# Moving 32 of 48 modulation blocks from VectorE and GpSimd into TensorE steps of a later scan

## The chip, the cores and the metric

One core of one Trainium2 chip runs the whole program. The metric is device microseconds of one execution; lower is better.

## The reference, cut to what matters

The program is two blocks of a network over 1024 tokens of width 1024. The first block has two layers (dilated attention beside a gated scan, then an HGRN scan). The second block is modulated by a condition vector, mixes a pooled branch, an SSD scan and a delta-rule scan (GDN), and ends in 16 experts. The modulation rows are what the change is about:

```python
sc = jax.nn.silu(c)              # c: 1 x 1024
scc = jax.nn.silu(c_ctx)[None]
m_lat = jnp.split(sc @ ada_w[l] + ada_b[l], 6, axis=-1)    # ada_w: 1024 x 6144
m_ctx = jnp.split(scc @ ada_w[l] + ada_b[l], 6, axis=-1)
h_lat = modulate(rms_norm(x, norm1_g[l]), m_lat[0], m_lat[1])
h_ctx = modulate(rms_norm(ctx, norm1_g[l]), m_ctx[0], m_ctx[1])
...
x = x + m_lat[2][:, None] * mix_lat
h_lat = modulate(rms_norm(x, norm2_g[l]), m_lat[3], m_lat[4])
x = x + m_lat[5][:, None] * expert_choice_ffn(h_lat, ...)
```

Columns 0 to 2047 of `ada_w` (shift and scale of the first norm) are needed for both condition vectors and early, by the context; columns 2048 to 6143 are needed for `c` alone and not before the mixers' output projection.

## The kernel before, in words

The kernel is written with a tile framework. The program text gives each instruction a priority by its place (earlier text first; `high_priority` lifts a stretch), and a planner puts the ready instruction of highest priority next on each engine's in-order queue, by its own estimate of durations. So work that stands later in the text runs early where it is ready, as filler. Tiles live in pools on a left and a right stack; a pool opened after another has closed takes its memory. Tiles of one tag share `bufs` buffers. PSUM banks are tags too: in the second block there are three banks `mm`, one `a`, two `o` and two `tr`.

The order of the text: the four heads of layer 0 (`Layer0.heads`, with `Gated` units on all engines and dense products of three passes, `mm3`, L135 to L141); after head 3, two `inputs` pieces and `modulation()`, which runs `ada`; then attention, the output projection, the context, HGRN with the context's work aside, the second projection; then `latent_mixers`: projections, `ssd`, three `gdn_scan` pairs hp = 0, 1, 2; then `MixersOut` in four groups, the router and the experts.

`ada` (L939) makes the 6144 columns in 48 blocks of 128. A block has two loads `aw` of 256 KB (L955, two buffers, 512-byte pieces). Where `j % 3 != 2` (two blocks of three), GpSimd scales the four k-slices by `c` (L966) and adds them up (L967, L969, L972); else VectorE does it in four accumulating instructions (L961, L963). The first 16 blocks do this for `c_ctx` too, always on VectorE. One TensorE product with a column of ones sums over the partitions (L978, PSUM tag `f` while `aside` is set), VectorE adds the bias (L979), and a store writes 128 columns to `mods` in DRAM (L980).

`gdn_scan` prepares both directions and returns `carry`, which walks 15 steps: eight small products into the one bank `a` (L1702) and one VectorE addition (L1704), each step waiting for the last, at high priority. `gdn_finish` (L1727) normalises, transposes, gates and stores. All text of `scan(0)` and of `ssd` stands before the first `carry`. The pools `ls` (SSD's tiles) and `lphs` close after `ssd`; `MixersOut.open` then opens `z2` in their place: `z` (8 x 4 KB per partition), `m2` from `mods`, weights and the inputs `yin`. A group of `MixersOut` is 96 products of 512 columns (8 token blocks x 2 halves x 2 chunks x 3 passes) and 16 additions into `z` (L1911).

## Time and profile before

| what | us |
|---|---|
| runs shown | 3608.28, 3609.12, 6455.0 |
| median of the runs | 3609.12 |
| the profiled execution | 3603.5 |
| its span, first to last instruction | 3601.4 |
| TensorE busy | 3217.0 (89%) |
| VectorE / ScalarE / GpSimd busy | 2527.6 / 1577.9 / 1383.2 |
| modulation, first to last load issue | 10.8 to 566.8 |
| SSD's last store and first load of MixersOut | 3011.9 and 3013.3 |

All stretches are in us from the start of the span. PE is TensorE's products, PEld its weight loads, DVE is VectorE, ACT ScalarE, POOL GpSimd, SP the engine that issues most DMAs. The row PEclk is the clock granted to TensorE as a share of full speed. Busy products overlap in TensorE's pipeline, so start-to-start distances are the better price of one.

### The profile page before, as it was taken

Reading aid. Unit: us, or ns where it says so; the run is one execution under the profiler, and the core shown is the slowest. Engines: PE = TensorE matmul, PEld = TensorE weight load, DVE = VectorE, ACT = ScalarE, POOL = GpSimd, SP = SyncE. Lnnn points to the kernel's source line nnn. Section 1 sums busy time; section 2 is a strip of 40 time slices with the busy share of each in tenths; the row PEclk is TensorE's granted clock in tenths of the full one; section 3 lists DMA queues with packets and bytes.
Section 4 is the critical chain, followed back from the end, with each engine's and each line's share of the span. In section 5 each row is a group of like instructions: output and inputs, shape, how many; then the busy total and the mean of one; then the engine's idle time right before and its main releaser. Section 6 shows DMA issues by size and latency. Waiting matters only on the chain.

```text
span 3601.4 us, 63422 instructions
## 1 busy us (share of the span) xinstructions
PE 3217.0 (89%) x23688; PEld 2585.4 (72%) x23688; DVE 2527.6 (70%) x5574; ACT 1577.9 (44%) x3344; POOL 1383.2 (38%) x1415
## 2 busy tenths in 40 slices
PE   7998898999979999999999989869897777849997
PEld 6887786766658878788887877656676666637765
DVE  4777664346685686987668677758996665578876
ACT  3444333544424454545546452235342432126765
POOL 4657673000043233433324331443222564335533
PEclk9999999999999999999999999879998888969999
DMA  5233344252343222111112234234345755668994
GB/s 183 77 92 92 95 130 144 80 190 75 100 140 99 64 68 58 55 60 52 41 49 68 66 134 136 82 88 120 103 131 142 168 148 173 230 193 317 378 348 156
DMA packets 374000, 461.27 MB, mean 128 GB/s; under 512 B 150419, under 2 KB 280723, under 8 KB 373692
## 3 DMA queue, kind: packets, MB, share of 16 engines
q1 hardware_dynamic: 359852, 407.93, 36.3%
q0 software_dynamic: 13840, 49.29, 4.4%
q8 instruction: 187, 3.06, 0.4%
q14 instruction: 121, 0.99, 0.1%
HBM read 357.57 MB, written 104.27 MB: 128 GB/s over the span
## 4 chain that ended last, share of the span: by engine, by line
PE 49%; DVE 22%; DMA 9%; issue 8%; POOL 7%; ACT 3%; SPq 2%; DVEq 0%; POOLq 0%; ACTq 0%
PE mm L139 10%; PE mm L140 9%; PE mm L141 9%; POOL aw L966 2%; PE a L249 2%; DVE cacc L1145 2%; PE a L406 1%; PE a L2041 1%; DMA aw<-in_ada_w_dram 1%; DMA srow<-rdsl 1%; PE a L141 1%; PE a L140 1%; PE o L225 1%; PE a L139 1%; POOL wlo L116 1%
## 5 line engine op out<-in xcount | busy, mean ns | idle before, releaser
L116 POOL TENSOR_TENSOR wlo<-wraw,whi 128x1024 fp32r<-128x1024 f32 (+1 forms) x131 | 328.3, 2510 | 525.6 <-ACT whi L115 513.2
L139 PE MATMUL mm<-x1h,whi 128*128 128x512 f32 x576 | 234.9, 408 | 3.3 <-DVE G L921 1.7
L140 PE MATMUL mm<-x1l,whi 128*128 128x512 f32 x576 | 233.4, 405 | 1.7 <-DVE x1l L133 1.7
L141 PE MATMUL mm<-x1h,wlo 128*128 128x512 f32 x576 | 233.5, 405 | 0.0
L139 PE MATMUL mm<-whi,x1h 128*128 128x256 f32 x768 | 221.8, 289 | 0.4 <-DVE G L921 0.4
L141 PE MATMUL mm<-whi,x1l 128*128 128x256 f32 x768 | 219.6, 286 | 0.0
L140 PE MATMUL mm<-wlo,x1h 128*128 128x256 f32 x768 | 219.0, 286 | 0.0
L2029 DVE TENSOR_TENSOR elo<-eraw,ehi 128x1024 fp32r<-128x1024 f32 x136 | 184.8, 1381 | 47.1 <-ACT ehi L2027 46.7
L2027 ACT CAST ehi<-eraw 128x1024 fp32r<-128x1024 f32 x160 | 165.5, 1051 | 99.6 <-PE a L141 35.9
L115 ACT CAST whi<-wraw 128x1024 fp32r<-128x1024 f32 (+1 forms) x131 | 136.1, 1040 | 153.9 <-PE mm L140 76.2
L140 PE MATMUL mm<-wlo,xh 128*128 128x256 f32 x640 | 184.2, 288 | 1.9 <-POOL wlo L116 1.9
L141 PE MATMUL mm<-whi,xl 128*128 128x256 f32 x640 | 184.4, 289 | 0.0
L139 PE MATMUL mm<-whi,xh 128*128 128x256 f32 x640 | 183.6, 288 | 0.9 <-DVE G L623 0.9
L139 PE MATMUL mm<-x2h,whi 128*128 128x512 f32 x400 | 166.9, 417 | 10.2 <-ACT cu L1134 5.6
L139 PE MATMUL mm<-whi,yin 128*128 128x512 f32 x352 | 151.4, 433 | 25.0 <-DVE z L824 14.0
L141 PE MATMUL mm<-x2h,wlo 128*128 128x512 f32 x400 | 164.3, 412 | 0.8 <-POOL wlo L116 0.8
L140 PE MATMUL mm<-x2l,whi 128*128 128x512 f32 x400 | 164.6, 411 | 0.0
L139 PE MATMUL mm<-xh,whi 128*128 128x512 f32 x336 | 138.6, 412 | 20.4 <-ACT whi L115 17.6
L966 POOL TENSOR_SCALAR aw<-aw,ac 128x128 f32<-128x128 f32 x256 | 123.7, 498 | 85.7 <-DMA aw<-in_ada_w_dram 41.6
L139 PEld LDWEIGHTS mm<-whi,x1h 128*128 128x128 f32 x768 | 146.7, 191 | 3.1 <-issue 1.0
L140 PEld LDWEIGHTS mm<-wlo,x1h 128*128 128x128 f32 x768 | 146.7, 191 | 0.6
L141 PEld LDWEIGHTS mm<-whi,x1l 128*128 128x128 f32 x768 | 146.8, 191 | 0.3
(747 smaller groups left out, 10317.0 us busy)
## 6 DMA issues: line engine op xcount, KB each, us to landing
eraw<-in_we_gate_dram SPq DMA_DIRECT2D x64, 512.0 KB
eraw<-in_we_up_dram SPq DMA_DIRECT2D x64, 512.0 KB
eraw<-in_we_down_dram SPq DMA_DIRECT2D x64, 512.0 KB
yin<-yd POOLq DMA_DIRECT2D x29, 1024.0 KB, 9.6
aw<-in_ada_w_dram SPq DMA_DIRECT2D x96, 256.0 KB
yd<-y_hl SPq DMA_DIRECT2D x80, 256.0 KB
wraw<-in_w_dram SPq DMA_DIRECT2D x25, 512.0 KB
wraw<-in_w_out_dram SPq DMA_DIRECT2D x24, 512.0 KB
```

The lines of the kernel that those rows point to most:

```text
L115: nc.scalar.copy(hi[:, :sz], raw[:, :sz])
L116: nc.gpsimd.tensor_tensor(lo[:, :sz], raw[:, :sz], hi[:, :sz].bitcast(F32), op=ALU.subtract)
L139: nc.tensor.matmul(ps, sh, mh, start=first and i == 0, stop=False)
L140: nc.tensor.matmul(ps, sh, ml, start=False, stop=False)
L141: nc.tensor.matmul(ps, sl, mh, start=False, stop=last and i == n - 1)
L225: nc.tensor.matmul(up[:, :Vd], kdT[:, i * P:(i + 1) * P], V[:, gi, :], start=True, stop=True)
L249: nc.tensor.matmul(ap[32 * c:32 * c + 32, o + lo:o + hi], sta[:, o + 32 * c:o + 32 * c + 32], mov[:, o + lo:o + hi], start=True, stop=True)
L406: nc.tensor.matmul(Ss[h][:, i * 256:i * 256 + w], q[hs[h], qc:qc + P], k[hs[h], lo:lo + w], start=True, stop=True)
L966: nc.gpsimd.tensor_scalar(w[:, k], w[:, k], at(k), 0.0, op0=ALU.mult, op1=ALU.add)
L1145: nc.vector.scalar_tensor_tensor(acc, u[:, i:i + n], cw[:, i:i + 1], acc, op0=ALU.mult, op1=ALU.add)
L2027: nc.scalar.copy(hi, raw)
L2029: nc.vector.tensor_sub(lo, raw, hi.bitcast(F32))
```

## The change

`ada` keeps the 16 blocks that both vectors need. The other 4096 columns move to a new generator `ada_rest`: 8 blocks of 512 columns, 8 k-steps each. A step loads 128 x 512 of `ada_w` (256 KB, 2 KB pieces, eight buffers) and issues four products, one per 32-column tile of the array: the stationary side is `c`'s slice in column 0 of a zeroed 128 x 32 tile, the moving side 128 columns of the weights, and tile q writes PSUM partitions 32q to 32q + 31. After eight steps one VectorE addition over 128 x 128 adds the bias, and one store writes 512 columns from partitions 0, 32, 64 and 96. `silu_c` (a load, three ScalarE and two VectorE instructions on 128 x 16) is now run in both places.

The generator is advanced one or two steps ahead of each step of `carry`, 22 times per scan, 66 in all for its 64 steps. Its pool `adb` is opened after `ls` and `lphs` have closed and is closed before `MixersOut` opens `z2`; the bank of its sums is `mm`.

```diff
+def ada_rest(g, pool, out):
+    nc, I = g.nc, g.I
+    c = silu_c(g, pool)
+    cz = pool.tile([P, 8, 32], F32, name="acz")
+    nc.vector.memset(cz, 0.0)
+    nc.vector.tensor_copy(cz[:, :, 0], c[:, 0])
+    b = pool.tile([P, P], F32, name="ab")
+    nc.vector.memset(b, 0.0)
+    for j in range(4, 12):
+        ps = g.psum("mm")[:, :P]
+        nc.sync.dma_start(b[0::32], dap(I["ada_b"], [[P, 4], [1, P]], j * 512))
+        for k in range(8):
+            w = pool.tile([P, 512], F32, name="aw", tag="aw", bufs=8)
+            nc.sync.dma_start(w, I["ada_w"][:, k, j * 512:(j + 1) * 512])
+            for q in range(4):
+                nc.tensor.matmul(ps[32 * q:32 * q + 32], cz[:, k], w[:, q * P:(q + 1) * P], start=k == 0, stop=k == 7)
+            if k < 7:
+                yield
+        r = pool.tile([P, P], F32, name="ar", tag="ar", bufs=2)
+        nc.vector.tensor_add(r, ps, b)
+        nc.sync.dma_start(dap(out, [[P, 4], [1, P]], j * 512), r[0::32])
+        yield
...
-    for j in range(6144 // n):
-        both = j < 2048 // n
+    for j in range(2048 // n):
...
-    def carry():
+    def carry(side=()):
+        side = iter(side)
...
         for i in range(m if fin is not None else m - 1):
+            for _ in range(1 + i % 2):
+                next(side, None)
             ps = g.psum("a")
...
-        for hp in range(3):
-            then = scan(hp + 1) if hp < 2 else None
-            gdn_finish(g, hp_, carry(), hp, fm_out["g", hp], Y)
-            carry = then
+        with g.pool("adb") as ap:
+            side = ada_rest(g, ap, z.mods)
+            for hp in range(3):
+                then = scan(hp + 1) if hp < 2 else None
+                gdn_finish(g, hp_, carry(side), hp, fm_out["g", hp], Y)
+                carry = then
+            for _ in side:
+                pass
         z.open()
```

## Rows read from the trace of the kernel before

**Rows 1.** Busy time of each engine by stage; columns as its first line says.
```profile
core 0: us, PE busy (x) PEld busy (x) DVE busy (x) ACT busy (x) POOL busy (x), PEclk, DMA share, GB/s
100.00:250.00 150.00, 149.59 (x1199) 128.47 (x1197) 120.03 (x333) 66.24 (x149) 84.31 (x114) 1.00 0.29 87
250.00:575.00 325.00, 294.65 (x2305) 247.45 (x2305) 220.09 (x574) 127.71 (x301) 232.23 (x363) 0.96 0.34 104
575.00:615.00 40.00, 29.25 (x149) 22.07 (x148) 15.83 (x37) 11.12 (x31) 12.87 (x12) 0.84 0.39 118
2770.00:3013.00 243.00, 175.78 (x2101) 155.83 (x2102) 156.57 (x268) 90.44 (x187) 145.65 (x122) 0.81 0.66 153
3013.00:3026.00 13.00, 9.22 (x169) 8.18 (x168) 7.64 (x16) 4.57 (x10) 9.56 (x8) 0.87 1.00 325
3026.00:3040.00 14.00, 8.35 (x85) 6.32 (x85) 4.73 (x12) 1.14 (x2) 0.00 (x0) 0.74 1.07 406
3013.00:3119.00 106.00, 82.18 (x665) 65.02 (x664) 58.27 (x100) 16.22 (x29) 33.38 (x28) 0.87 0.69 224
3119.00:3180.00 61.00, 60.45 (x346) 47.17 (x346) 34.53 (x75) 19.52 (x44) 21.64 (x22) 1.00 0.54 212
```

**Rows 2.** The chain that ended last in 250 to 575, shares by line.
```profile
by line: POOL aw L966 18.5%; DMA aw<-in_ada_w_dram 13.8%; issue 10.1%; DVE aacc L963 5.1%; PE mm L139 5.0%; PE mm L140 4.5%; PE mm L141 4.4%; POOL aw L967 4.4%; POOL wlo L116 3.0%; POOL aacc L972 2.7%; POOL aacc L969 2.3%; POOL u_qh L239 2.
```

**Rows 3.** Busy time in 250 to 575: tile `aw`'s instructions, then line L978's alone.
```profile
250.00:575.00 325.00, 40.83 (x96) 155.61 (x286) 0.96 0.34 104
...
250.00:575.00 325.00, 13.11 (x68) 3.04 (x68) 0.96 0.34 104
```

**Rows 4.** What TensorE waited for in 250 to 575: total us, times, longest.
```profile
PE a L214 <- DVE u_kd L210: 7.1, 5, 2.9
PE f L978 <- POOL aacc L972: 4.6, 5, 1.4
PE a L249 <- POOL u_qh L239: 4.5, 5, 2.6
...
PE f L978 <- POOL qdb L241: 0.8, 1, 0.8
PE f L978 <- DVE aacc L963: 0.5, 1, 0.5
```

**Rows 5.** Tile `aw` over the whole span: ns min/median/max, first and last start.
```profile
L966 POOL TENSOR_SCALAR aw<-aw,ac x256: 363/374/2561, 21.1 to 562.9; 128x128 f32<-128x128 f32 x128
```

**Rows 6.** SP's issues in order of time, 3010 to 3022.
```profile
3011.88 1.39 SPq L1355 DMA_DIRECT2D yd<-shl  x3
3013.31 0.50 SPq L1881 DMA_DIRECT2D m<-mods  x1
3015.50 6.07 SPq L1904 DMA_DIRECT2D z<-x2d  x8
```

**Rows 7.** The chain that ended last, 240 to 620: start, us, what.
```profile
376.05 1.94 DMA mods<-ar
378.34 2.80 DMA aw<-in_ada_w_dram
```

**Rows 8.** TensorE in order of time, 549.1 to 550.1: column tiles, then full-array products.
```profile
549.44 0.36 PE L249 MATMUL a<-u_qh,u_kh 128*32 128x64 f32 x6
549.73 0.50 PE L141 MATMUL mm<-xh,wlo 128*128 128x512 f32 x1
550.07 0.40 PE L139 MATMUL mm<-xh,whi 128*128 128x512 f32 x1
```

**Rows 9.** The chain that ended last, 2760 to 3110: eight fp32 products of 128x128 by 128 columns.
```profile
2870.53 2.00 PE tr L1649 x8
```

**Rows 10.** TensorE in 3013 to 3119 by line: busy, mean ns, idle before.
```profile
L139 PE MATMUL mm<-mhi,yin 128*128 128x512 f32 x76 | 32.3, 430 | 12.8 <-DMA yin<-yd 12.0 <-ACT mhi L1897 0.6 <-DVE z L1911 0.2
```

**Rows 11.** TensorE in order of time: products of MixersOut, then steps of scan 2.
```profile
3028.67 0.39 PE L140 MATMUL mm<-mlo,yin 128*128 128x512 f32 x1
3028.90 0.40 PE L141 MATMUL mm<-mhi,yin 128*128 128x512 f32 x1
3033.99 0.70 PE L1702 MATMUL a<-hB,hA 64*64 64x64 f32 x8 [0.40 <-DVE hB L1704]
3035.09 0.70 PE L1702 MATMUL a<-hB,hA 64*64 64x64 f32 x8 [0.40 <-DVE hB L1704]
```

**Rows 12.** GpSimd and SP in order of time, around 2755 and 2773.
```profile
2755.92 1.81 POOL L1528 MEMSET hwb<- 128x2048 f32 x1 [0.97 <-DVE gH L1492]
...
2773.15 0.34 SPq L1518 DMA_DIRECT2D gT<-gR  x1
```

More of the change, by code (lines that the diff above doesn't have):

```diff
@@ L936, with silu_c @@
 EPS2 = 1e-6
+def silu_c(g, pool):
+    c = pool.tile([P, 2, 8], F32, name="ac")
+    sg = pool.tile([P, 2, 8], F32, name="acs")
+    g.nc.sync.dma_start(c, g.I["c2"])
+    sigmoid(g, sg, c)
+    g.nc.vector.tensor_mul(c, c, sg)
+    return c
+def ada_rest(g, pool, out):
[20 more added lines that the diff above has]
+        yield
 def ada(g, pool, out):
     nc, I = g.nc, g.I
-    c = pool.tile([P, 2, 8], F32, name="ac")
-    sg = pool.tile([P, 2, 8], F32, name="acs")
-    nc.sync.dma_start(c, I["c2"])
-    sigmoid(g, sg, c)
-    nc.vector.tensor_mul(c, c, sg)
+    c = silu_c(g, pool)
     ones = pool.tile([P, 1], F32, name="aones")
@@ L949, in ada @@
     n = 128
-    for j in range(6144 // n):
-        both = j < 2048 // n
-        acc = [pool.tile([P, n], F32, name=f"aacc{v}", tag=f"aacc{v}", bufs=1) for v in range(1 + both)]
+    for j in range(2048 // n):
+        acc = [pool.tile([P, n], F32, name=f"aacc{v}", tag=f"aacc{v}", bufs=1) for v in range(2)]
         for kh in range(2):
@@ L955, in ada @@
             nc.sync.dma_start(w, I["ada_w"][:, 4 * kh:4 * kh + 4, j * n:(j + 1) * n])
-            for v in ((1, 0) if both else (0,)):
+            for v in (1, 0):
                 at = lambda k: c[:, v, 4 * kh + k:4 * kh + k + 1]
@@ L972, in ada @@
                         nc.gpsimd.tensor_add(acc[v], acc[v], w[:, k])
-        for v in range(1 + both):
+        for v in range(2):
             r = pool.tile([1, n], F32, name="ar", tag="ar", bufs=1)
```

## The prediction, as it was put on record

> **What bounds the kernel now.** TensorE is busy for 3217 of 3601 us, so the first view is the table of stages, read for where TensorE is not busy and who is. Beside the modulation it shows two pictures [rows 1]: full from 100 to 250 (149.6 of 150 us), but 30.4 us idle from 250 to 575, with GpSimd at 71%. In this second part all 32 blocks that the change moves are made. The chain of waits there runs through them: GpSimd's scaling, the loads and the additions of `aw` make some 47% of it [rows 2]. A chain share is no gain, since TensorE is 91% busy beside it, so the third view is what TensorE itself waited for [rows 4]: 5.9 us for the modulation's sums, and 7.1 and 4.5 us for `u_kd` and `u_qh`, which VectorE and GpSimd make between modulation instructions. Where the work goes, TensorE is 72% busy and the DMA engines 66% from 2770 to 3013, while SSD and the scans run; from 3119 to 3180 TensorE is full [rows 1]. What starts the last stretch is the order of loads: SSD's last store, then at once `m2`, the weights and `z` [rows 6].
>
> **Early part, what goes.** In 250 to 575 `aw` costs GpSimd 155.6 us and VectorE 40.8 us, and L978 costs TensorE 13.1 us in 68 instructions [rows 3]. Nearly all is moved work (32 products of two instructions are 64 of the 68). Sure is the product time, 13.1 x 64/68 = 12.3 us, and the 5.9 us of waits on these sums. Of the other 24.5 us of idle I take a quarter, 6 us: the waits for `u_kd` and `u_qh` (11.6 us) have two causes, the queue of their engine and the length of their own chain, and I give the queue half. Sum 24 us. Ends: 8 us, if the gated units' chain sets the end, as from 575 to 615, where TensorE idles 10.8 of 40 us with no modulation product left but one [rows 1]; and 12.3 + 30.4 = 43 us if all idle time goes.
>
> The scaling instruction takes 374 ns in the median, but up to 2561 ns, and 155.6 us over 286 instructions of `aw` is far above the median [rows 3, 5]: GpSimd is held up while VectorE works. The Trainium skill (SBUF — State Buffer, section "SBUF: two separate sides") says why: GpSimd and a VectorE instruction with two SBUF inputs use one port pair under an exclusive lock, held for a whole instruction. By that rule VectorE gets back what it waits as well, and the early gain would go towards its upper end, 43 us; no row here separates VectorE's wait for a lock from its work.
>
> Removed at no gain: 64 loads and 64 small transfers from SP's queue, and 16.8 MB from a stage whose DMA share is 0.34 [rows 1]; the first 250 us keep their work.
>
> **Late part, what comes.** 64 loads of 256 KB (16.78 MB), 256 products, which are 512 instructions as fp32 takes two, 8 additions, 8 bias loads, 8 stores. When can they start? Memory is waited for tile by tile: `hwb`, a tile of the scans' pool, was cleared at 2755.9, once the one old tile beneath it had been read, 17 us before the last store from the same old pool [rows 12]. But `adb` lies where SSD's tiles lie, and, by the order of tiles in the text, most of its eight load buffers cover tiles that SSD reads to its last chunks. `z2` lies there too, and all its loads came after SSD's last store, at 3013 [rows 6]. I take 3013 for `adb` as well.
>
> Then the loads set the pace. Two neighbouring stretches with saturated DMA moved 325 and 406 GB/s [rows 1], so 16.78 MB take 52 or 41 us; I take 46. A load's latency (2.8 us), and the last block's addition and store (a `mods` store took 1.9 us), make 5 us [rows 7]. Other loads that run in the same stretch (before, 13 us at 325 and 14 us at 406 make 9.9 MB, less `z`'s 4.2 MB) cost 6 of some 15 us that they would need alone, as most wait for `m2`. `ada_rest` ends at 3013 + 46 + 5 + 6 = 3070.
>
> Its products beside that: six on column tiles took 0.29 us from first start to the next other product [rows 8], 0.05 us each, so 512 take 25 us, under the loads. The upper end is the full-array price, 2.00/8 = 0.25 us [rows 9], 128 us in all. I take the first, since it is the same 128x32 form. The additions (0.3 us), clearing `cz` and `ab`, and the second `silu_c` lie beside the first loads; without that cover they would cost 5 us.
>
> Who waits: on SP an `aw` load waits for the products eight loads before it, and behind it stand the scans' `hS` and gate loads and the stores of `gdn_finish`. On TensorE a product waits for its load, and behind it stand the steps of scan 2, 1.1 us each [rows 11]; 15 steps, some 17 us, fit into the 57 us. On the bank side a sum holds one of three `mm` banks for eight steps. The heavy wait is a new one: `z` lies over `adb`, so it can't be loaded before `ada_rest` is done, and no sum of MixersOut can leave PSUM before.
>
> What the end then is: MixersOut's 384 products start 0.23 us apart [rows 11], 89.5 us. By 3119 the old kernel had done 3 x 76 = 228 of them [rows 10]; the other 156 are 36.4 of the 60.5 us busy in 3119 to 3180 [rows 1], leaving 24.1 us for transposes and router. From 3070: 2.5 us until `z`'s first tile, 89.5 + 24.1 us, less three banks done ahead (18 x 0.23 = 4.2 us), plus 6 us for imperfect packing. That ends at 3188, against 3180. Only 8 us are lost, as the old kernel idles TensorE for 24 of 106 us from 3013 [rows 1]; the scan steps move into the wait. What is late next is the choice of experts and their products, unchanged and shifted.
>
> **Sum.** 3603.5 - 24 + 8 = 3587.5 in the profiled run's terms. The median of the runs shown is 5.6 us above that execution, so the forecast is 3593 us.
>
> **Rivals.** *The loads crawl* (slower). `z` is held by `ada_rest`'s end, so every microsecond of loading beyond 3070 is lost in full. The late part eats the early gain when it ends at 3086, with 62 us for the loads, 16.78 MB at 271 GB/s. For it: the stages around moved 153 and 212 GB/s [rows 1], though not for lack of bandwidth in the second, and the expert weights may be fetched as soon as the scans' memory is free, ahead of `z`. Against it: the two saturated stretches. At 212 GB/s the loads take 79 us: 33 us more, 3626 us. At 153 GB/s, 110 us, it is 3657.
>
> *Blocks hide inside SSD.* One or two buffers cover tiles that SSD frees early, and waits go tile by tile [rows 12]. If most blocks are done by 3013, the late part costs nothing but crowding: 3585 us, and less if TensorE's idle time there shrinks. Against: all of `z2`'s loads waited for SSD's last store [rows 6].
>
> *The early stage doesn't shrink.* The gated units' chain sets its end, gain 8 us: 3609 us. For it: VectorE's chain instructions are no fewer, and 10.8 us idle remain at its tail. Against: the full stage from 100 to 250, with the same chain.
>
> *Four tiles are no four.* The products run one after another at the full-array price: 128 us instead of 46, 82 us more, 3675 us. Against: the column-tile rows [rows 8].
>
> *Changing the shape costs.* After column tiles, the first full-array product of the trace starts its successor 0.34 us later instead of 0.23 [rows 8, 11], 0.11 us; two changes per generator step, 128 in all, make 14 us, 3607 us if none hides under loads. The Trainium skill (TensorEngine Tiling (Array Packing), "Key Properties") says that a change of tiling mode drains TensorE, and here 128x32 tiles would alternate with the scans' 64x64 and MixersOut's full array; by its rule the price stands at every change, by the trace it is 0.11 us.
>
> **How the numbers follow.** Chances: forecast 0.42, loads crawl 0.22, hidden in SSD 0.14, no early gain 0.14, shape 0.05, tiles in a row 0.03. The likeliest one's own range is 3575 to 3611 (41 to 52 us of loads, early gain 14 to 30). The whole range is 3564 to 3642: below, the early gain's upper half with the forecast's late part, or hidden blocks; above, the middle of the crawling loads. A measurement of this kernel tells 2% (72 us) from no change: below 3537 needs the whole 43 us early and as much late (0.02); above 3681 needs the loads at the bottom rate and no early gain (0.04); within it 0.94.
>
> **What would show it.** Right: in the changed profile TensorE idles at most 15 us over what is left of the stage now at 250 to 575, attention starts some 24 us earlier, `aw` loads of 256 KB run back to back for about 50 us right after SSD's last store, and `z`'s first load comes right behind the last `mods` store. Wrong: loads of `aw` well before SSD's end; a stretch in which TensorE waits for `aw` with scan steps queued behind; `z` loaded more than 75 us after SSD's last store; or an attention start that hasn't moved. The forecast fails most easily by the planner: a new order on SP or TensorE in stages that the change doesn't touch.

## The result, and the profile after

| | before | after |
|---|---|---|
| median of the runs, us | 3609.12 | 3629.27 |
| ratio after / before | | 1.0072, 95% interval 1.0058 to 1.0087 |
| the profiled execution, its span | 3603.5, 3601.4 | 3629.27, 3627.5 |
| attention's first instruction (tile `spread` is cleared) | 611.1 | 569.8 |
| SSD's last store | 3012.8 | 2967.1 |
| last modulation store of `ada_rest` | | 3042.8 |
| MixersOut: first and last sum into `z` | 3046.8, 3171.6 | 3065.8, 3195.5 |
| experts: first one-hot tile | 3230.9 | 3255.2 |

The kernel became slower by 0.7%, 26 us by the ratio (20 between the two medians): clear of the spread, though less than 2%. One disturbed run of before (6455) stands outside the ratio. SSD's last store is the last of three; the 3011.9 given ahead of the prediction is the first of them. The table tells where: a lead of 41 us at attention, 46 us at SSD's end, and a lag of 24 us at MixersOut's last sum, which stays to the end. So 70 us are lost between 2967 and 3196, more than the early part wins.

**The early part.** Busy time by stage, in the columns of [rows 1]. The stretch from 250 to 575 now ends at 535:

```profile
core 0: us, PE busy (x) PEld busy (x) DVE busy (x) ACT busy (x) POOL busy (x), PEclk, DMA share, GB/s
250.00:535.00 285.00, 274.39 (x2242) 240.19 (x2241) 157.30 (x451) 127.17 (x298) 99.29 (x90) 0.98 0.18 59
535.00:571.00 36.00, 24.78 (x136) 19.05 (x135) 15.27 (x36) 11.66 (x33) 9.11 (x11) 0.85 0.32 107
```

TensorE's idle time fell from 30.4 to 10.6 us and its busy time by 20.3, together the 40 us. What it still waits for there, the first two of four lines (total us, times, longest), against [rows 4]:

```profile
PE tr L314 <- DVE s_y L291: 7.0, 3, 3.4
PE a L214 <- DVE u_kd L210: 1.7, 3, 1.0
```

The waits for `u_kd` fell from 7.1 to 1.7 us, and that for `u_qh` is gone. More happened than a shorter queue: the same VectorE instructions became shorter. Groups of VectorE by line, before (250 to 575) and after (250 to 535), busy and mean ns:

```profile
L187 DVE TENSOR_TENSOR u_kb<-u_b 128x256 f32<-128x256 f32 x21 | 12.4, 591 | 0.5
L180 DVE TENSOR_TENSOR_SCAN u_b<-reset,gm 128x256 f32<-128x256 f32 x12 | 11.0, 917 | 0.3
```
```profile
L187 DVE TENSOR_TENSOR u_kb<-u_b 128x256 f32<-128x256 f32 x20 | 8.5, 425 | 0.7
L180 DVE TENSOR_TENSOR_SCAN u_b<-reset,gm 128x256 f32<-128x256 f32 x11 | 7.6, 690 | 0.3
```

One form on one tile takes 591 ns in the mean beside a GpSimd that is busy for 71% of the stage, and 425 beside one at 35%. The mean hides how it comes about. The same line before, ns min/median/max:

```profile
L187 DVE TENSOR_TENSOR u_kb<-u_b x21: 404/426/2433, 250.5 to 557.4; 128x256 f32<-128x256 f32 x21
```

The median is the same as after; a few instructions take much longer, one of them 2433 ns (the other 20 have a mean of 499). In the trace, the six of the 21 with no GpSimd instruction beside them took 406 to 425 ns, with as much DMA traffic around them as the others had; all nine above 426 ns had one beside them, and six that had one were not slower. The Trainium skill (SBUF — State Buffer, section "SBUF: two separate sides") states the lock between the two engines that the prediction weighed; these rows agree with it. The gain came near the upper end of 43 us, though not by the sum that gave that end, since 10.6 us of idle time remain.

**The late part.** SP's issues in order of time, against [rows 6]:

```profile
2964.05 3.51 SPq L1386 DMA_DIRECT2D yd<-shl  x6
...
2969.62 0.43 SPq L964 DMA_DIRECT2D aw<-in_ada_w_dram  x1
...
3042.78 0.49 SPq L971 DMA_DIRECT2D mods<-ar  x1
3043.33 0.43 SPq L1919 DMA_DIRECT2D m<-mods  x1
...
3045.44 2.50 SPq L1942 DMA_DIRECT2D z<-x2d  x5
...
3080.86 0.90 SPq L2059 DMA_DIRECT2D eraw<-in_we_gate_dram  x2
...
3097.93 37.33 SPq L1933 DMA_DIRECT2D mraw<-in_w_out_dram  x6
```

The order is the one foretold: late loads right behind SSD's last store, `m2` and `z` right behind the last modulation store. The sizes are not: 73 us from the first late load to the last modulation store, and the last six weight loads of MixersOut stand behind 14 loads of expert weights (3081 to 3097). The tile `aw` over the span (ns min/median/max, first and last start), and who waited for it (us, times):

```profile
L966 PE MATMUL mm<-aw,acz x512: 272/297/423, 2973.8 to 3042.1; 128*32 128x128 f32 x171
...
L964 SPq DMA_DIRECT2D aw<-in_ada_w_dram x64: 327/382/1524, 2969.6 to 3035.9; - x64
...
PE mm L966: 14.7, 23
```

Busy time by stage of the late part, then pieces of it: one amid the late loads, the others through MixersOut:

```profile
2967.10:3042.80 75.70, 58.25 (x1039) 38.54 (x1040) 22.27 (x53) 8.94 (x21) 11.10 (x8) 0.80 0.87 292
3042.80:3195.50 152.70, 121.80 (x580) 93.62 (x577) 77.03 (x124) 25.32 (x47) 43.10 (x38) 0.89 0.56 201
...
2985.00:3005.00 20.00, 13.54 (x228) 8.54 (x228) 4.50 (x9) 2.32 (x4) 1.50 (x3) 0.63 1.04 372
...
3043.00:3060.00 17.00, 7.52 (x67) 4.99 (x62) 7.01 (x7) 2.65 (x4) 6.59 (x4) 0.75 0.91 339
3060.00:3080.00 20.00, 16.29 (x59) 12.34 (x59) 11.10 (x18) 3.25 (x6) 5.83 (x5) 0.78 0.85 258
3080.00:3100.00 20.00, 13.24 (x55) 10.22 (x54) 13.32 (x22) 2.38 (x4) 6.51 (x6) 0.90 0.97 340
3100.00:3120.00 20.00, 12.14 (x39) 9.14 (x39) 5.93 (x9) 1.24 (x2) 2.88 (x2) 0.76 0.62 224
3120.00:3140.00 20.00, 16.91 (x67) 13.38 (x68) 8.73 (x13) 1.14 (x2) 3.96 (x4) 0.92 0.37 132
3140.00:3160.00 20.00, 20.00 (x89) 16.52 (x88) 11.45 (x17) 1.24 (x2) 2.56 (x2) 0.99 0.00 1
```

TensorE stands idle for 31 of the 153 us from the last modulation store to the last sum, all of it ahead of 3140, and its clock is at 0.75 to 0.92 there. What it waited for between 3045 and 3140, and then the chain that ended last, in order of time:

```profile
PE mm L139 <- ACT mhi L1935: 10.2, 2, 5.9
PE mm L139 <- DVE z L1949: 8.6, 6, 2.5
PE mm L139 <- DMA yin<-yd: 8.4, 2, 5.3
```
```profile
3052.16 9.52 DMA mraw<-in_w_out_dram
...
3085.57 12.28 DMA eraw<-in_we_up_dram
3097.93 14.59 DMA mraw<-in_w_out_dram
...
3130.92 5.34 DMA yin<-yd
```

The chain reads as the queue does: a weight load that shares the DMA engines with `z`, then an expert load, then a weight load of 14.59 us behind the expert loads, then inputs. These last inputs were not issued before 3130.92 because their buffer was not free: GpSimd, which issues them, stood 13.9 us for TensorE's products (`PE mm L141`). So part of this chain is MixersOut's own buffers and not the queue.

### The profile page after: what moved, and what is told of

It reads as the page before. It is cut to its first block, busy times and chain, and to the rows that moved or that the text cites. A ratio compares the mean times of both kernels' runs of the same rounds, so it can differ in the third digit from the quotient of the medians.

```text
span 3627.5 us, 63825 instructions
## 1 busy us (share of the span) xinstructions
PE 3229.6 (89%) x24136; PEld 2595.5 (72%) x24136; DVE 2481.9 (68%) x5467; ACT 1579.9 (44%) x3347; POOL 1245.1 (34%) x1142
## 4 chain that ended last, share of the span: by engine, by line
PE 56%; DVE 20%; DMA 9%; issue 7%; POOL 3%; ACT 3%; SPq 2%; DVEq 0%; POOLq 0%; ACTq 0%
PE mm L139 11%; PE mm L140 11%; PE mm L141 11%; PE a L249 2%; DVE cacc L1176 2%; DMA aw<-in_ada_w_dram 1%; PE o L225 1%; PE a L406 1%; PE a L2079 1%; PE a L140 1%; PE a L141 1%; DVE elo L2067 1%; DMA srow<-rdsl 1%; PE a L139 1%; DVE gtmp L1496 1%
## 5 line engine op out<-in xcount | busy, mean ns | idle before, releaser
L141 PE MATMUL mm<-x1h,wlo 128*128 128x512 f32 x576 | 232.4, 404 | 0.0
L141 PE MATMUL mm<-whi,x1l 128*128 128x256 f32 x768 | 219.6, 286 | 0.0
L141 PE MATMUL mm<-whi,xl 128*128 128x256 f32 x640 | 182.8, 286 | 0.0
L239 POOL TENSOR_TENSOR u_qh<-u_qa,facY 128x256 f32<-128x256 f32 x64 | 68.1, 1064 | 293.4 <-DVE u_qa L236 272.0
L141 PE MATMUL mm<-x2h,wlo 128*128 128x512 f32 x400 | 163.0, 408 | 0.8 <-POOL wlo L116 0.8
L239 POOL TENSOR_TENSOR u_qh<-u_qa,facX 128x256 f32<-128x256 f32 x64 | 67.0, 1046 | 245.5 <-DVE u_qa L236 193.7
```

The source lines that it names most:

```text
L141: nc.tensor.matmul(ps, sl, mh, start=False, stop=last and i == n - 1)
L239: nc.gpsimd.tensor_tensor(v3(qh, 32), v3(qa, 32), bcast(fqh, nck, 32), op=ALU.mult)
```

## The experiments

Each stands beside fresh runs of the kernel before. Theory A, as first written: MixersOut's start is held by the late part (its memory lies over `adb`, its loads stand behind the late ones), and TensorE has used up the scan steps that covered that start. Theory B: the bytes moved between SSD's last store and MixersOut's third group set the time. Theory C: the planner loses the early gain on the way. Theory D: the 512 products are the price.

**Early half alone.**

```diff
-        with g.pool("adb") as ap:
-            side = ada_rest(g, ap, z.mods)
...
+    nc.sync.dma_start(dap(out, [[4096, 1], [1, 4096]], 2048), dap(I["ada_b"], [[4096, 1], [1, 4096]], 2048))
```

> The early half alone: the 32 blocks are gone from the early part and nothing takes their place late; the 4096 late columns of the modulation get their bias only, by one transfer, so their products are left out. Theory A (the early gain is whole and the loss is all late): TensorE enters attention 40 us earlier, as in the changed kernel, and keeps it to the end, 3609 - 40 = 3569 us, between 3563 and 3573. The forecast's own term: 24 us, 3585. Theory C (the early gain is lost again on the way, by a new order of the planner): over 3600.

Measured: 3577.69 us beside 3605.59, ratio 0.992 (0.9899 to 0.9942): 29 us. In its trace attention starts 39 us earlier and SSD's last store is 36 us earlier, but MixersOut's last sum only 23:

```profile
L1946 DVE TENSOR_TENSOR z<-z,mm x64: 673/687/690, 3012.2 to 3148.4; 128x512 f32<-128x512 f32 x64
...
L1737 PE MATMUL a<-hB,hA x336: 217/219/367, 2825.7 to 3059.9; 64*64 64x64 f32 x168
...
3104.52 0.61 PE L2225 MATMUL o<-rw,shb 128*128 128x16 f32 x2 [12.21 <-DVE shb L2224]
```

The scans' last step, the second line, in the kernel before and in the changed one:

```profile
L1702 PE MATMUL a<-hB,hA x336: 218/267/367, 2846.3 to 3060.1; 64*64 64x64 f32 x168
```
```profile
L1736 PE MATMUL a<-hB,hA x336: 218/218/367, 2817.4 to 3035.0; 64*64 64x64 f32 x168
```

With the early half alone the scans end at 3059.9, where before had them end at 3060.1. A lead at SSD's end is worth less at MixersOut, with no late work at all. The trace shows where much of it goes. MixersOut starts early, and scan 2 now walks among its products, from 3008 to 3060 (3031 to 3060 before). The router's rows are loaded only behind the scans' last stores, at 3092 (3093 before). By then MixersOut's third group is done, and its fourth stands in TensorE's queue behind products with those rows (`shb`): TensorE waits 15.0 us for them, 12.21 in the third line. (MixersOut's last weights, on the same queue of SP behind the rows, are loaded at 3104; what the rows alone cost is not told apart.) The gain is between the forecast's 24 and the 40 seen at attention; C has its part, though not the whole.

**Late half alone.**

```diff
-    for j in range(2048 // n):
+    for j in range(6144 // n):
...
+            side = ada_rest(g, ap, g.dram.tile([8 * D], F32, name="spare"))
```

> The late half alone: all 48 blocks stay early, and the 64 steps with their loads, products, additions and stores run in the scans as well, into a spare tensor, so that the work is done twice. Theories A and B (the loss is late): 3609 + 65 = 3674 us, between 3665 and 3685. The forecast's term of 8 us: 3617. Theory C: under 3640.

Measured: 3673.81 us, ratio 1.0181 (1.0156 to 1.0206): 68 us more. The forecast's term of 8 us falls; the loss is late. The halves don't simply add: 68 less the 28 or 29 of the early half alone is 40 us, and the whole change loses 26.

**`z` not held, first try.**

```diff
         with g.pool("adb") as ap:
+            ap.tile([P, 19776], F32, name="apad")
...
-            w = pool.tile([P, 512], F32, name="aw", tag="aw", bufs=8)
+            w = pool.tile([P, 512], F32, name="aw", tag="aw", bufs=4)
```

> The pool of the late part begins with an unused tile of 77 KB, so that its four load buffers (four instead of eight, for room) lie at the top of the memory that MixersOut takes, over the third buffer of its inputs and the end of the first, and not over the residual rows z and the weights. Theory A (MixersOut's start is held until the last modulation store, and then runs bare): z's loads are issued before the last modulation load, and the end comes 25 to 45 us earlier than the changed kernel, 3585 to 3602 us. Theory B (the 16.8 MB themselves hold the DMA engines, whoever waits): z's and the weights' loads share the engines with them, at most 10 us earlier, 3617 or more. With four buffers the loads could go slower, which would cost up to 20 us in both.

Measured: 3650.51 us, ratio 1.0123 (1.0102 to 1.0144), slower still. SP in order of time:

```profile
3060.64 0.52 SPq L971 DMA_DIRECT2D mods<-ar  x1
...
3063.58 5.96 SPq L1943 DMA_DIRECT2D z<-x2d  x8
```

`z` still came behind the last modulation store, so the run didn't test what it was made for. It did show a price of four buffers at their new place: 85 us from SSD's last store to the last modulation store instead of 76.

**Eight loads instead of 64.**

```diff
+            if j == 4:
+                ws.append(pool.tile([P, 512], F32, name=f"aw{k}"))
+                nc.sync.dma_start(ws[k], I["ada_w"][:, k, j * 512:(j + 1) * 512])
+            w = ws[k]
```

> Only the first eight of the 64 late loads are made; the other 56 steps multiply the same eight tiles again, so that 7 of 8 blocks of the late modulation are wrong numbers of the same size. All products, additions and stores stay. Theory B (the loads set the late part's length, each microsecond of them is lost): the last modulation store comes 35 to 40 us earlier, and so does the end, 3587 to 3592 us or below. Theory A (the start of MixersOut is bare after any late part, because the scan steps are walked together with it): the store comes 30 us earlier, the 22 us between z's first load and its first sum remain, 3595 to 3600 us. Theory D (512 products of a new form are the price): within 10 us of the changed kernel, 3619 or more.

Measured: 3598.86 us, ratio 0.9981 (0.9971 to 0.9991); against the changed kernel's 1.0072 that is 33 us.

```profile
L974 SPq DMA_DIRECT2D mods<-ar x8: 491/494/536, 2978.9 to 3008.2; - x8
...
L1952 DVE TENSOR_TENSOR z<-z,mm x64: 667/687/689, 3032.2 to 3157.0; 128x512 f32<-128x512 f32 x64
```

The last store is 35 us earlier, and so is the last sum (38). 24 us from store to first sum remain, as A had it; the end lies at A's 3600, the move at B's size, so the run doesn't choose between them. It does show that the loads are what turns the gain into a loss: without them the version is slightly faster than the kernel before, with all products still there, so D falls.

**The late loads on GpSimd's queue.**

```diff
-            nc.sync.dma_start(w, I["ada_w"][:, k, j * 512:(j + 1) * 512])
+            nc.gpsimd.dma_start(w, I["ada_w"][:, k, j * 512:(j + 1) * 512])
```

> The 64 late loads are issued by GpSimd instead of SP, nothing else is touched. With z's memory free its loads still stood behind the last late load on SP; this run takes SP's order away and leaves the memory as it is. If SP's order alone held z (A2): z, the weights and the first inputs are loaded some 30 us earlier, 3600 to 3610 us. If the memory alone holds it (A1): z's first load still comes after the last product has read its tile, within 5 us of the changed kernel, 3624 to 3634 us, though weights may be there sooner. Theory B: unchanged, 3629 us.

Measured: 3626.9 us, ratio 1.0058 (1.0037 to 1.0078), within 5 us of the changed kernel. SP's order alone is not the price.

**Both, by unused tiles.**

```diff
+    pool.tile([P, 11280], F32, name="apad")
     c = silu_c(g, pool)
...
+            w = pool.tile([P, 512], F32, name="aw", tag="aw", bufs=4)
+            nc.gpsimd.dma_start(w, I["ada_w"][:, k, j * 512:(j + 1) * 512])
```

> Both at once: GpSimd issues the late loads, and the late pool is laid by unused tiles over the third buffers of MixersOut's weights and inputs, so that z, the weights and the inputs of its first group are free; four load buffers instead of eight, one result tile instead of two. Theory A (bare start, by memory and queue together): z is loaded while the late loads run, its first sum comes before the last modulation store or within 5 us of it instead of 23 us after, and the end is 20 to 30 us earlier than the changed kernel, 3600 to 3610 us. Theory B (the DMA engines are full, so whatever is loaded sooner delays the rest): 3620 us or more; the four buffers alone could add up to 20 us in both.

Measured: 3655.91 us, ratio 1.0132 (1.0111 to 1.0154). `m2` again was loaded only behind the last modulation store (3093.6, 119 us after SSD's last store), and `z` behind it. Why the planner held it there with free memory and its two blocks stored at 3006 wasn't found, so this run too says nothing on A. It wasn't the data alone: in the late half alone, whose late stores go to a spare tensor, `m2` was loaded behind the last of them all the same (3086.2 behind 3083.4).

**MixersOut opened first, its buffers lent.**

```diff
-        with g.pool("adb") as ap:
-            side = ada_rest(g, ap, z.mods)
+        z.open()
+        side = ada_rest(g, z.zp, z.mods, z.ready)
...
+    y = pool.tile([P, 2, T], F32R, name="yin", tag="yin", bufs=3).bitcast(F32)
+    l = pool.tile([P, D], F32R, name="mlo", tag="mlo", bufs=3).bitcast(F32)
...
+        if j == 5:
+            ready()
```

> MixersOut's pool is opened first and the late part borrows from it (one weight buffer for the small tiles, one input and one weight buffer as six load buffers), GpSimd issues the late loads, z is loaded ahead of them, and m2 is loaded as soon as its two blocks are stored. So neither z nor the weights nor the first inputs wait for the last of the late work; all of it is still done. The two runs with unused tiles in the pool left z behind the last store all the same, so they had not tested this. Theory A (the start of MixersOut is bare because it is held): its first sums come beside the late loads, at most 10 us after the last modulation store, and the end is 20 to 40 us earlier than the changed kernel, 3590 to 3610 us. Theory B (the DMA engines are the limit, the same bytes pass between SSD's last store and MixersOut's third group): the sums start earlier, but the end moves by less than 10 us, 3620 us or more.

Measured: 3635.01 us, ratio 1.0087 (1.007 to 1.0104).

```profile
L978 SPq DMA_DIRECT2D mods<-mhi x8: 502/506/542, 3003.1 to 3096.5; - x8
...
L1959 DVE TENSOR_TENSOR z<-z,mm x64: 669/687/690, 3063.4 to 3200.3; 128x512 f32<-128x512 f32 x64
```

Now the first sum stands 33 us ahead of the last modulation store, so the start isn't held, and the last sum is where it was (3200 against 3196). That is B's number, and A's gain didn't come. But the run is no clean test: the late part took 130 us instead of 76, and MixersOut's later inputs waited for the lent buffers (one load of `yin`, at 3082.7, stood 12.6 us for the late products).

**Fewer products at equal loads.**

```diff
-            for q in range(4):
+            for q in range(4 if k in (0, 7) else 1):
```

> All 64 late loads stay, but six of each eight steps make one product instead of four (224 of 512 instructions are left), so that three of four rows of each late sum miss six of their eight slices. Theory B (loads and the bytes behind them set the late part): the last modulation store moves by less than 8 us and the end by less than 10, 3620 us or more. Theory D (the products' time on TensorE, 288 instructions at 0.05 to 0.08 us, and the changes of tile shape around them are the price): 15 to 23 us earlier, 3606 to 3614 us.

Measured: 3635.58 us, ratio 1.0079 (1.0061 to 1.0098): no change from the changed kernel. With 224 instructions instead of 512 the last store is at 3041.6 and the last sum at 3195.1:

```profile
L971 SPq DMA_DIRECT2D mods<-ar x8: 492/514/567, 2981.8 to 3041.6; - x8
...
L1949 DVE TENSOR_TENSOR z<-z,mm x64: 623/687/690, 3064.5 to 3195.1; 128x512 f32<-128x512 f32 x64
```

The products lie under the loads, as the forecast had it.

**No expert prefetch under MixersOut.**

```diff
-    turns = cycle(rps)
+    turns = cycle(rps[1:])
```

> The changed kernel with the experts' weights loaded only into the 13 buffers that come free after the router, so that none of their 7 MB moves while MixersOut runs; the experts then start late, and their first weights are not hidden, so that the whole time says nothing. Theory B (bytes: the prefetch stands ahead of the last weights of MixersOut on SP and on the DMA engines): from the last modulation store to MixersOut's last sum it takes 15 to 25 us less than the 153 us of the changed kernel. If MixersOut's pace there is set by TensorE or by the splitting of its weights: within 8 us of 153.

Measured: 3610.72 us, ratio 1.0011 (0.9998 to 1.0023), by the ratios 22 us less than the changed kernel; the whole time does say something, since the experts lost nothing.

```profile
L971 SPq DMA_DIRECT2D mods<-ar x8: 492/510/542, 2980.2 to 3041.3; - x8
...
L1949 DVE TENSOR_TENSOR z<-z,mm x64: 667/687/690, 3065.5 to 3181.8; 128x512 f32<-128x512 f32 x64
```

From the last store to the last sum it takes 140.5 us instead of 152.7. That is 12 us, below B's 15 to 25 and above the 8 of the other case: a collision that is real, and smaller than B said. Another 8 us come behind the router: from the first one-hot tile to the span's end it takes 364.3 us instead of 372.3. Those 8 have nothing to do with the change: every version without the prefetch takes 364 to 367 us there, and every other one 369 to 373.

**The kernel before without prefetch.** The same diff, on the kernel before.

> The kernel before, with the experts' weights loaded only into the 13 buffers that come free after the router. In the changed kernel this took 12 us out of MixersOut and some 20 out of the whole. If the collision of the prefetch with MixersOut's weights was made by the change (it brought the prefetch 30 us ahead of MixersOut's last weights): the kernel before gains nothing, 3600 to 3612 us. If the collision was there before and the change only kept it: the kernel before gains as much, 3580 to 3590 us, and the change costs its 25 us with or without it.

Measured: 3599.28 us beside 3606.21, ratio 0.9988 (0.9975 to 1.0001): some 4 us, at most 9. MixersOut's last sum is not earlier (3175.2); 6 us come behind the router (364.6 us instead of 370.5). So the collision in MixersOut came with the change.

**Opened first, and no prefetch.** The two diffs together.

> The run that opens MixersOut early and lends its buffers to the late part, now also without the early prefetch. Theory A (the start is held; the prefetch only ate what an early start won): clearly faster than the changed kernel without prefetch (3611), by 10 to 25 us, 3586 to 3601 us. Theory B (bytes between SSD's last store and MixersOut's third group): the same as it, 3605 to 3618 us.

Measured: 3612.43 us, ratio 1.0016 (1.0004 to 1.0029), the same as without the early start (3610.72). A's gain doesn't come here either, with the collision out of its way but the lent buffers still in it.

**The late part elsewhere.** Inside SSD, and inside the second output projection:

```diff
+        for _ in range(4):
+            next(side, None)
         xb = tokens(c)
```
```diff
+        with g.pool("adb") as ap:
+            side = ada_rest(g, ap, mods)
             for c in range(0, 8, 2):
                 out1.group(c, c + 1)
+                g.aside = "f"
+                for _ in range(16):
+                    next(side, None)
```

> The late part is moved forward into SSD: its pool lies beneath SSD's (seven load buffers for room), four steps stand ahead of each of SSD's 16 chunk steps, and nothing is left for the scans. In the changed kernel that stage (2735 to 2967) leaves TensorE 72 of 232 us idle and the DMA engines a third. Theory A (the late part hurts because it stands between SSD and MixersOut, whose start then runs bare): the work hides in SSD but for 10 to 20 us, 3585 to 3600 us, against some 3577 without any late work. Theory B (16.8 MB cost their time wherever other loads run): 40 us or more over that, 3617 us or more.

> The late part is moved further forward, into the second output projection (2150 to 2320 in the changed kernel, TensorE idle for 38 of 170 us, DMA share 0.34): 16 steps behind each of its first four groups, the sums in the bank f that lies unused there. Theory A: the loads hide, the products cost what TensorE has not idle there, at most 10 to 15 us over some 3577, so 3580 to 3592 us. Theory B: the loads hold up that projection's inputs and weights on the same queue for their 57 to 75 us less its idle share, 3610 us or more. A third case: the products stand in a stretch that is full and cost their whole time on TensorE, 26 to 41 us, 3603 to 3618 us.

Measured: 3603.74 us, ratio 0.9994 (0.9982 to 1.0007), and 3606.0 us, ratio 0.9994 (0.9984 to 1.0005). Both cost some 27 us over no late work (0.9994 against 0.992) and give the early gain back whole. In SSD that lies between the theories; in the projection the time is that of the third case, products in a stretch that has no room for them, though products and loads were not told apart there. In SSD its last store moves from 2976.4 without late work to 3005.8; in the projection SSD's first load moves from 2737.5 to 2773.1 (in an execution that took 10 us longer than the median). The scans' place costs 55 us by the same sum.

**Half of the change.**

```diff
+    for j in range(4096 // n):
...
+    for j in range(8, 12):
```

> Half of the change: blocks 0 to 31 stay early as before, and only the last four late blocks of 512 columns (32 loads, 256 instructions) run in the scans. If the late cost goes with its loads and the early gain with its blocks (the changed kernel lost about 65 us late and won 40 early): 20 early, 33 late, 3609 + 13 = 3622 us. If the first blocks removed bring most of the early gain, because they take the queue of VectorE and GpSimd below TensorE's pace: 35 early, 33 late, 3607 us. If the late cost is mostly the bare start and not the loads: 20 early, 45 late, 3634 us.

Measured: 3608.28 us beside 3604.21, ratio 1.0004 (0.999 to 1.0017). Attention starts 20 us earlier, half of the whole gain, so it doesn't saturate, and the second case has the time for a wrong reason: the late half costs only what the early half wins. So the late cost grows faster than its bytes: half of them cost 15 to 20 us, all of them 55.

**The old form, during attention.**

```diff
+            g.aside = "mm"
+            for _ in range(8):
+                next(late)
+            g.aside = None
```

> A version without the late part: the 32 blocks keep their form of before (GpSimd scales and adds, one product with ones, one addition), but are made during attention, eight behind each pair of heads, all on GpSimd, which is busy for 28 of 405 us there. No new loads fall between SSD and MixersOut. If the early gain is whole and attention has room: 32 products of 0.27 us and little else, 3578 + 9 = 3587 us, 3580 to 3592. If GpSimd's work slows VectorE in attention (186 us of GpSimd beside a VectorE that is busy for 60%): 20 to 30 us more, 3600 to 3612 us.

Measured: 3725.43 us, ratio 1.0331 (1.0302 to 1.0361), far outside both cases. TensorE's waits between 575 and 1050:

```profile
PE mm L982 <- POOL aacc L976: 60.5, 10, 11.8
```

The products with ones stand at high priority in TensorE's queue, they wait for GpSimd's sums, and everything behind them waits too. The first output projection, whose sums had filled attention's gaps from 761.1 on, makes its first sum at 1030.6; it shares the bank `mm` with the products. How the loss divides between the two was not tested. I had priced GpSimd's time and not the place in the queues.

**Combinations without prefetch.** The diffs of SSD and of the half, each with that of the prefetch:

> The late part inside SSD (which took as long as the kernel before) and no early prefetch. If both are separate: 3604 - 20 = 3584 us, faster than both kernels. If the prefetch collided only because of the late part's loads between SSD and MixersOut, which are gone here: no gain, 3600 to 3608 us.

> Half of the change (16 of the 32 blocks moved, 8.4 MB late, into the scans) and no early prefetch. If the prefetch's price is the same 20 us in every version: 3608 - 20 = 3588 us. If it goes with the late bytes: half of it, 3598 us.

Measured: 3587.88 us beside 3606.21, ratio 0.9952 (0.9934 to 0.9969), and 3599.8 us, ratio 0.9979 (0.9966 to 0.9991). The first is faster than both kernels, by 17 us than the one before, with all of the work done. What its second case assumed holds, since the stretch from SSD's end takes the same time with and without the prefetch (table below), and still there is a gain: in the traces 7 us of it lie behind MixersOut's last sum, as in every version, and 4 ahead of SSD's last store. The half, too, gains 7 us behind the last sum and nothing in the stretch, so it has the time of "half of it" for another reason.

```profile
L1389 SPq DMA_DIRECT2D yd<-shl x24: 359/506/2891, 2891.1 to 3002.0; - x24
...
L1954 DVE TENSOR_TENSOR z<-z,mm x64: 669/686/689, 3035.8 to 3160.0; 128x512 f32<-128x512 f32 x64
```

## Why the prediction was wrong

The time of the stretch from SSD's last store to the first row block that MixersOut finishes (its first store to `accd`), in the profiled executions; the bytes are the stretch's rate times its length:

| kernel | us | MB |
|---|---|---|
| before | 124.8 | 29.6 |
| early half alone | 143.5 | 27.4 |
| eight loads | 158.2 | 32.3 |
| changed, no prefetch | 182.6 | 39.6 |
| changed | 194.4 | 47.0 |
| fewer products | 193.9 | 46.9 |
| opened first | 199.5 | 47.1 |
| half of the change | 160.0 | 38.6 |
| half, no prefetch | 162.9 | 31.3 |
| late part in SSD | 124.3 | 27.7 |
| in SSD, no prefetch | 124.0 | 20.5 |

The 69.6 us from before to changed can be read as three differences between runs: 18.7 that the early half alone loses, 14.7 more with the products and steps but few loads, 36.2 more with the loads. Without the expert weights 11.8 of them go. They are not three causes that add: the wait for the router's rows, 15.0 us in the early half alone, is 1.2 us in the changed kernel.

Nor do the bytes alone set the time, as B would have it. In two pairs of the table the expert weights are 7 MB of the stretch and cost it nothing: in half of the change and with the late part in SSD, where 14 expert loads also stand ahead of the last weights. A collision was seen behind the full late part alone.

**Early gain, 24 us: right in kind, too small.** It was 41 us at attention. TensorE's busy time fell by 20.3 us, where I had 12.3 for the products (its granted clock rose from 0.96 to 0.98 in the stage), and its idle time by 19.7, where I had 12. Of the waits for `u_kd` and `u_qh`, which I halved, 9.9 of 11.6 us went; VectorE's own instructions became shorter too. At the end of the whole program the gain is 29 us (early half alone), by accident near the term. One reading was wrong: 155.6 us over 286 instructions is not far above the median, since 374 ns is the median of L966 alone and the 286 are of four lines with medians of 374 to 738 ns (the first stands in [rows 5]). At these medians they make some 129 us, and what GpSimd was held up is nearer to 27 us.

**Start of the late loads at SSD's last store: right.** 2.5 us behind it.

**57 us to the end of `ada_rest`: mis-sized.** It took 75.7. The loads alone ran 72 us, 232 GB/s where I took 365; the stretch moved 292 GB/s with all its other loads, below both saturated rows that I took as bounds [rows 1]. TensorE waited 14.7 us for `aw`. This is the rival of the crawling loads, at its mild end, and the run with eight loads prices the loads at 33 us of the whole.

**The products at 0.05 us: near enough, in part by luck.** The row that it came from has products of 64 columns, the new ones have 128. TensorE in order of time, the third row at the lower level of the clock:

```profile
2983.56 0.64 PE L966 MATMUL mm<-aw,acz 128*32 128x128 f32 x16
2984.14 0.49 PE L1680 MATMUL tr<-hke,hwb 128*128 128x128 f32 x2
...
3001.89 0.66 PE L966 MATMUL mm<-aw,acz 128*32 128x128 f32 x8 [0.57 <-DMA aw<-in_ada_w_dram]
...
3009.84 0.43 PE L966 MATMUL mm<-aw,acz 128*32 128x128 f32 x8 [0.41 <-DMA aw<-in_ada_w_dram]
3010.20 0.46 PE L1736 MATMUL a<-hB,hA 64*64 64x64 f32 x8
3010.58 0.43 PE L966 MATMUL mm<-aw,acz 128*32 128x128 f32 x8
```

Sixteen take 0.58 us to the next start of another shape, eight between scan steps 0.36. So eight more cost 0.22 us, 0.03 each, and the remaining 0.14 go with entering and leaving the shape: 9 us for 64 such pairs, all under the loads, as the run with fewer products shows. Single starts in the trace agree: the four tiles' products start 7 ns apart, and the next four 0.11 us later. The rivals of four tiles that are no four, and of the changing shape, fall.

**"Only 8 us are lost ... the scan steps move into the wait": the step that failed.** I let MixersOut run at TensorE's pace once `z` could be loaded: 2.5 us to its first tile, 0.23 us per product, 6 us for packing, which makes 109 us to its last sum (the 118 to 3188, less the 8 that lie behind the last sum). It took 152.7, 43 us more and the largest error. The kernel before could have warned me: from `m2`'s load to the last sum it took 158 us itself (3013.3 to 3171.6). I added up TensorE's work and let the stage shrink by 49 us because TensorE idles there and the scan steps leave; in the run it shrank by 6, so that the later opening moved nearly whole into the end. TensorE was idle for 31 us and not 8, and most of the other 20 us are longer products: the 384 products took 102 us from start to start, idle time taken off, where I had 85, and the granted clock is 0.75 to 0.92 up to 3140 and 0.99 behind. The waits are for weights, inputs and sums: the scan steps that had filled such gaps lay under the late loads (the last at 3035.0), and the loads of 3043 to 3100 (339, 258 and 340 GB/s) bring `z`, weights, inputs and expert weights through the same engines. That the collision is a cause is shown (no prefetch: 12 us, and none in the kernel before). That the filler's absence is one is argued only, and one trace speaks against it: with the late part in SSD the scans end 19 us behind SSD's last store instead of 47, and the stretch takes 124.3 us as in the kernel before. What set the rest of the 152.7 stays open.

**"The heavy wait is a new one": seen, but no price.** `z` did wait for `ada_rest`. But opening MixersOut first took the wait away and gave nothing, with or without prefetch, though it held other buffers in its place.

**The median, 5.6 us above the profiled run**: no matter here; the changed kernel's profiled run is its median.

Sum in the forecast's terms: 22 us better at SSD's end, 19 worse for the loads, 43 for MixersOut, 2 behind it, 42 in all: 3587.5 + 42 = 3629.5 against the measured 3629.27. The likeliest case and its sign were wrong. That the whole range held the time is luck in good part: its upper end was made of crawling loads, which cost 19 us, while the 43 us of MixersOut were in no rival and the early gain made up for half of them. The likeliest case's own range doesn't follow from its terms either, which give 3582 to 3609 us. Of what I listed as signs, two came out on the wrong side: TensorE waited for `aw` with scan steps queued behind, and `z` was loaded 78 us after SSD's last store, where 75 was the mark.

What stays open: what sets MixersOut's length from its opening, whether the late loads cost their time by holding `z` or by the DMA engines that they share, and why `m2`'s load stayed last in the runs with unused tiles.

## What to carry to other kernels

A stage with an idle TensorE is no free place for work whose loads take longer than the idle time: price moved work at its new place by its loads, beside everything that is loaded there for the next stages, and price the next stage by the time that it took from its own opening, not by TensorE's work in it alone. A prefetch that was free can collide once something else moves in ahead of it, and is worth one run without it. A moved instruction's own time can be the smallest part of its price: with the old form during attention the work lay on a nearly idle GpSimd, and the kernel became 121 us slower than before, with TensorE's products waiting for GpSimd's sums.

## What the runs showed of the hardware beyond that

- VectorE's 128x256 instructions on SBUF took 591 ns in the mean beside a busy GpSimd and 425 beside a quieter one, a scan 917 and 690 ns; the medians of the first hardly differ (426 and 425), and single ones took up to 2433 ns.
- A stall cost twice: from 2985 to 3005 TensorE waited for loads and was busy for 13.54 of 20 us, and its granted clock was 0.63. Eight column-tile products took 0.66 us at the lower level (1.2 GHz) where they took 0.43 at the full one (2.4 GHz).
- Whether SP or GpSimd issued the 64 late loads made no difference (3629 and 3627 us). Four load buffers instead of eight, at another place, cost 9 us over 64 loads of 256 KB.
- Four fp32 products on four column tiles started 7 ns apart, and 0.11 us apart from the next four, at the full clock; 0.14 us went with entering and leaving the shape.
- Expert weights loaded 120 us later, behind the router, cost the experts nothing: 364 us from the first one-hot tile to the end, against 372 with the prefetch; in the kernel before 365 against 371.
